# RWKV-7 time mixing: two solve copies one step later, one more weight ahead in two phases, the scan's second loads and its PSUM layout earlier

## The chip, the cores and the metric

The program runs on one core of a Trainium2 chip. The metric is the device time of one execution in microseconds (us), and a kernel's time is the median of its runs. Inside the core TensorE (PE) multiplies matrices, VectorE (DVE), ScalarE (ACT) and GpSimd (POOL) do the work by element, and SyncE (SP) issues most of the DMA transfers. Every engine works through its own instructions in a fixed order and stops at the first whose inputs are not there.

## The reference, cut to what matters

A decoder trunk of two layers on one sequence of 1024 positions, width 1024. Each layer has a token mixer, a cross-attention into 256 memory tokens and a squared-ReLU MLP, each with a norm ahead and behind. Layer 0 mixes by a gated linear recurrence, layer 1 by RWKV-7, which is what the change touches:

```python
xx = x_prev - x
r = (x + xx * mu[0]) @ w_rkv[0]
k = (x + xx * mu[2]) @ w_rkv[1]
v = (x + xx * mu[3]) @ w_rkv[2]
...
def step(state, inp):
    r_t, w_t, k_t, v_t, a_t, b_t = inp
    sa = jnp.einsum('bhij,bhj->bhi', state, a_t)
    state = state * w_t[:, :, None, :] + sa[..., None] * b_t[:, :, None, :] + v_t[..., None] * k_t[:, :, None, :]
    y_t = jnp.einsum('bhij,bhj->bhi', state, r_t)
    return state, y_t
```

There are 16 heads of 64. All numbers are float32.

## The kernel before

**Products in three parts.** A float32 product is made of three matmuls (mm3, L318 to L320): each operand is split into a rounded high part (ACT, L233) and a remainder (DVE, L234). So every weight and every activation passes through one ACT and one DVE instruction before PE can use it. A 128x128 block against 512 columns costs three matmuls.

**The order of work.** The program writes instructions down in an order; a planner then simulates the engines with its own durations, and issues on each engine what is ready, earliest written first. `with self.behind()` queues what is written in the block behind the last instruction written before it on each engine. A tile of the pool `u` (45 tiles of 128x1024) is handed out when the planner finds one free.

**The phases of layer 1's mixer** (function `rwkv`). After the low-rank maps come three phases, in which PE makes 8 blocks f = 0 to 7 of 128 features each, for k, then r, then v. `fphase` (L584 on) makes one block: 16 times three matmuls into the PSUM tile p, of which there are two, and then an evacuation: `prep_head` for k (ACT L1349, DVE L1350), `evac_r` for r (DVE L1519), `evac_v` for v (ACT L1553 and what follows). The input of each phase is a mix of x and its predecessor, `rwkv_make_mix`: in four steps for each half of the positions, ACT scales (L1217), DVE adds (L1220), and both split (L233, L234). The mix for r is made while k's blocks 6 and 7 are on PE and after them; the mix for v likewise at the end of the r phase. Mixes written into `self.later` are taken up in the middle of a block.

**Weights.** `take` (L262 on) hands out the next weight of a list known beforehand. At each call it issues loads up to `depth + ahead` weights beyond the one taken, and splits up to `depth` beyond it. In these phases DA = (2, 1), so two are split and one more is loaded.

**Aside steps.** Each block ends a step, numbered 0 to 6 for k (the last has blocks 6 and 7), 7 to 12 for r, 13 to 19 for v. `aside(step)` (L1488) places there the pieces of the chunk solve: the 64x64 triangular systems of all heads, in four groups q = 0 to 3. `solve_load` fetches a group, `solve` works through 31 dependent pairs of instructions (L1433, L1435), on POOL for q = 0, 1, 2 and on DVE for q = 3, and `solve_store` makes a transposed copy on ACT (L1445) and stores both (SP, L1446 and L1447). merge_load, merge and merge_store (steps 9 to 18) build the full inverses from these. The tuples SL, SO and ST give the steps of load, solve and store for q = 0 to 3.

**The scan.** 16 chunks c of 64 positions follow each other; a chunk's state update needs the chunk before. `load(n)` fetches the operands of chunks 2n and 2n+1: two `u` tiles by four DMAs (L1624), two halves of a z tile (L1627), and a `u` tile without a DMA; `load_solved(n)` the inverses (L1638, from what merge_store wrote), `load_late(n)` the values and gates (L1651, L1655). While chunk c runs, `scan_scale`, `scan_gram` (PE, L1679) and `scan_keys` prepare chunk c+1. Afterwards `tphase` multiplies by w_o into PSUM tiles p.

**PSUM.** "mixed" keeps four single banks (pool `still`) and two p tiles of two banks; "banks" turns the p tiles into four more banks. `bank(n)` takes from the one pool or from the other in turn. A pool can be laid out anew when the last reader of its old tiles is done.

Of the kernel before, what the change touches and what calls it, by code (L numbers as in the profile page):

```python
# [1141 lines left out]

TURNS = [[f] for f in range(6)] + [[6, 7]]

SL, SO, ST = (2, 5, 8, 9), (2, 5, 8, 9), (5, 8, 12, 13)
ML, ME, MS = range(9, 17), range(10, 18), range(11, 19)
SE = [lambda nc: nc.gpsimd] * 3 + [lambda nc: nc.vector]
MQ = lambda nc, f: nc.sync if f < 4 else nc.gpsimd
DA = (2, 1)
# [112 lines left out]
def rwkv(self, X, xt, lw_wa, lw_g, post, mid):  # L1262
# [116 lines left out]
    def sums(f):  # L1379

        ps = sm[f] = self.bank()
        for tt in range(8):
            self.between.append(lambda tt=tt: mm(ps[:, tt * 2:tt * 2 + 2], st_k[f][0][:, tt * 128:tt * 128 + 128], self.ind,
                                                 start=True, stop=True))
# [113 lines left out]
    for i, fs in enumerate(TURNS):  # L1498
        for f in TURNS[i + 1] if i < 6 else []:
            decay(f)  # L1500
        if len(fs) > 1:

            self.later.append(lambda: rwkv_make_mix(self, X, 0, 0, xr[0], range(2)))
        if i:
            sums(fs[0] - 1)
        self.fphase(I["b_w_rkv"][0, 1], fs, xk, prep)
        if 0 < i < 6:
            gram(fs[0] - 1)
        aside(i)
# [3 lines left out]
    def early(f):  # L1513
        ld[f] = self.unit()
        nc.sync.dma_start(ld[f], Pd[f * 128:f * 128 + 128, :])
# [6 lines left out]
    for i, fs in enumerate([[0, 1], [2], [3], [4], [5], [6, 7]]):  # L1522
        for f in fs:
            early(f)
        if i == 5:
            self.later.append(lambda: rwkv_make_mix(self, X, 3, 0, xv[0], range(3)))
        if i in (1, 2):
            sums(5 + i)
        self.fphase(I["b_w_rkv"][0, 0], fs, xr, evac_r, spread=i == 0)
        if i == 0:  # L1530
            prep_rest(7)
        if i in (1, 2):
            gram(5 + i)
        aside(len(TURNS) + i)
# [75 lines left out]
    def load(n):  # L1610

        if n >= 8:
            return
        ts = slice(n * 128, n * 128 + 128)
        if n in (0, 2):
            t = self.half_big([2, 8, 2, 128])
            mvb.extend(t[:, i] for i in range(2))
        mv = mvb[n % 4]
        sts = []
        for g in range(2):  # L1620
            st = self.unit().rearrange("p (e q w t) -> p e q w t", e=2, q=4, w=2)
            for e in range(2):
                es = slice(n * 128 + e * 64, n * 128 + e * 64 + 64)
                nc.sync.dma_start(st[:, e], STd[:, 4 * g:4 * g + 4, :, es])  # L1624
            sts.append(st)
        for w in range(2):
            nc.sync.dma_start(mv[:, :, w, :], MVd[:, :, w, ts])  # L1627
        pcs = self.unit().rearrange("p (e q t) -> p e q t", e=2, q=8)
        for e in range(2):
            c, cs = 2 * n + e, slice(e * 64, e * 64 + 64)  # L1630
            cst[c] = dict(st=[t[:, e] for t in sts], mv=mv[:, :, :, cs],
                          pcs=pcs[:, e], pcc=self.pc[:, c * 8:c * 8 + 8].unsqueeze(2), gw=[])

    def load_solved(n):
        if n >= 8:
            return
        xu = self.unit().rearrange("p (q t) -> p q t", t=128)
        nc.sync.dma_start(xu, XTd[:, :, n * 128:n * 128 + 128])  # L1638
        for e in range(2):
            cst[2 * n + e].update(xt=xu[:, :, e * 64:e * 64 + 64])  # L1640
# [101 lines left out]
    for i, fs in enumerate(turns):  # L1742
        for f in turns[i + 1] if i < 6 else []:
            early(f)
        if fs[-1] >= 5:
            self.depth, self.ahead = min(2, 7 - fs[-1]), 0
        self.fphase(I["b_w_rkv"][0, 2], fs, xv, evac_v, spread=i == 0)
        aside(len(TURNS) + 6 + i)
        if fs[-1] == LD:
            with self.behind():  # L1750
                load(0)
        if fs[-1] == 6:
            load_solved(0)
    for c in range(2):
        scan_scale(c)
        for g in range(2):
            scan_gram(c, g)
            scan_mask(c, g)
            scan_keys(c, g)
    load_late(0)  # L1760
    self.psum_layout("banks")
    for h in range(2):
        nc.gpsimd.memset(cst[0]["sv"][hr[h], :, h, :], 0.0)
    for c in range(16):
        if c % 2 == 0:
            with (ExitStack() if c else self.behind()):
                load(c // 2 + 1)
                load_solved(c // 2 + 1)
                load_late(c // 2 + 1)
        s = cst[c]  # L1770
        sv, mv, pcc, xtc, pcs = s["sv"], s["mv"], s["pcc"], s["xt"], s["pcs"]
        dbv = self.db[:, 0:128].rearrange("p (q a t) -> p q a t", a=2, t=8)[:, :, c % 2, c // 2:c // 2 + 1]
        W, U, S, wsb = [], [], [], []
        y = self.unit()
        yp = self.bank(c)
        Y = yp.rearrange("p (q i) -> p q i", i=64)

        def values(m):

            ph = self.bank(m)  # L1780
            reg = [ph[:, x * 256:x * 256 + 256].rearrange("p (q i) -> p q i", i=64) for x in range(2)]
            W.append(reg[0]); U.append(reg[1]); S.append(reg[0])
            for q, h in heads:
                mm(W[m][hr[h], q, :], s["gw"][m][:, q, h, 0:64], sv[:, m * 4 + q, h, :], start=True, stop=True)
            w_ = y[:, 512 + m * 256:768 + m * 256].rearrange("p (q i) -> p q i", i=64)
            nc.scalar.copy(w_, W[m])
            wsb.append(w_)

        def decayed(m):
            for h in range(2):  # L1790
                nc.gpsimd.tensor_tensor(pcs[hr[h], m * 4:m * 4 + 4, :], sv[hr[h], m * 4:m * 4 + 4, h, :],
                                        pcc[hr[h], m * 4:m * 4 + 4].broadcast_to([64, 4, 64]), ALU.mult)

        def from_state(m):
            for q, h in heads:
                mm(Y[hr[h], m * 4 + q, :], mv[hr[h], m * 4 + q, 1, :], sv[hr[h], m * 4 + q, h, :],  # L1796
                   start=(m == 0 and q == 0), stop=False)

        def solved(m):
            qs = slice(m * 4, m * 4 + 4)  # L1800
            for q, h in heads:
                mm(U[m][hr[h], q, :], xtc[hr[h], m * 4 + q, :], wsb[m][hr[h], q, :], start=True, stop=True)
            for h in range(2):
                nc.vector.tensor_tensor(sv[hr[h], qs, h, :], U[m][hr[h]], dbv[hr[h], qs].broadcast_to([64, 4, 64]), ALU.mult)

        def update(m):
            qs = slice(m * 4, m * 4 + 4)
            for q, h in heads:
                mm(S[m][hr[h], q, :], s["gk"][:, m * 4 + q, h, :], sv[:, m * 4 + q, h, :], start=True, stop=True)
            for h in range(2):  # L1810
                nc.vector.tensor_add(cst[c + 1]["sv"][hr[h], qs, h, :], pcs[hr[h], qs, :], S[m][hr[h]])

        def output():
            for m in range(2):
                for q, h in heads:
                    mm(Y[hr[h], m * 4 + q, :], s["gw"][m][:, q, h, 64:128], sv[:, m * 4 + q, h, :], start=False,
                       stop=(m == 1 and q == 3))
            nc.scalar.copy(y[:, 0:512], yp)
            s["y"] = y


        todo = [(decayed, 0), (decayed, 1)] if c < 15 else []
        if c:
            todo += [(scan_scale, c + 1)]
        todo += [(values, 0), (from_state, 0), (values, 1), (from_state, 1)]
        if c:
            todo += [(post_var, c - 1)]
        todo += [(solved, 0), (solved, 1)]
        if c > 1:
            todo += [(flip_out, c - 2)]  # L1830
        if c:
            todo += [(scan_gram, c + 1, 0)]
        if c < 15:
            todo += [(update, 0), (update, 1)]
        if c:
            todo += [(scan_keys, c + 1, 0), (scan_keys, c + 1, 1), (scan_mask, c + 1, 0), (scan_gram, c + 1, 1), (scan_mask, c + 1, 1)]
        todo += [(output,)]
        if c:
            todo += [(post_norm, c - 1)]
        for fn, *args in todo:  # L1840
            with self.line("scan"):
                fn(*args)
        if c > 4 and c % 2:

            n = (c - 3) // 2
            self.depth, self.ahead = max(0, n - 4), min(n, 4)
            self.fetch(self.taken - 1)
    post_var(15)
    post_norm(15)
    self.depth, self.ahead = 2, 3  # L1850
    self.psum_layout("mixed")

    self.later += [lambda: flip_out(14), lambda: flip_out(15)]
    w = I["b_w_o"][0]
# [54 lines left out]
```

## Time and profile before

| what | value |
|---|---|
| median of 3 runs (lowest to highest) | 2872.57 us (2865.99 to 2873.09) |
| the profiled execution's own time | 2871.51 us |
| its span, first to last instruction | 2869.8 us |
| granted TensorE clock over the span | 0.993 |
| PE busy / idle | 2779.0 us / 90.8 us |
| POOL solve of q = 0 / 1 / 2, first to last instruction | 1422.5 to 1476.6 / 1484.2 to 1540.9 / 1546.5 to 1588.4 |
| phases k, r, v on PE | about 1356 to 1486, 1489 to 1599, 1604 to 1749 |
| scan's chunks on PE | about 1762 to 1920 |

How to read the rows: a timeline row gives start and duration in us, the engine, the line, the operation, out<-in with shapes, and a count when neighbours are merged; in brackets stands the idle time of the engine just before, and what ended it. PEld is the weight load of a matmul, SPq the queue of SP, on which only DMA issues stand. A row of waits gives the total, the number and the longest. A row of a window gives busy time for each engine (with the number of instructions), the clock granted to PE, the mean busy share of the 16 DMA engines and GB/s. Tile names carry no numbers: u is the pool of 128x1024 tiles, p and q are PSUM, z the larger tiles, d scratch in DRAM.

### The profile page before, as it was taken

The page shows a single profiled execution, that of the slowest core. Times are in us where ns is not written, and L with a number is a line of the kernel's source. Part 1 is how long each engine was busy: PE and PEld are TensorE (multiplying, and loading weights), DVE is VectorE, ACT ScalarE, POOL GpSimd, SP SyncE. Part 2 cuts the span into 40 slices and gives each one's busy share as a digit, 9 for nine tenths or more (in the row PEclk, how much of TensorE's full clock was granted, in tenths as well). Part 3 has the DMA queues.
Part 4 walks back from the last instruction along what each step waited for, and adds up shares of the span by engine and source line. Part 5 has one row for each costly group of instructions (what it writes and reads, how often), then busy time and mean ns, then how long its engine had stood idle before and what let it go on. Part 6 is the DMA issues. An engine that isn't in the chain of part 4 may idle for free.

```text
span 2869.8 us, 42738 instructions
## 1 busy us (share of the span) xinstructions
PE 2779.0 (97%) x16955; PEld 2320.8 (81%) x16955; DVE 1845.2 (64%) x2004; ACT 1431.3 (50%) x2203; POOL 913.3 (32%) x962
## 2 busy tenths in 40 slices
PE   7999999999999999998999898999999999999998
PEld 6888788888888888887777687888888888888886
DVE  5577556557455577886575834785665655467778
ACT  5456344546544543438562544663463644555333
POOL 2000114023666500013188223863303276640001
PEclk9999999999999999999999999999999999999999
DMA  8212352323445654433557798963132255464453
GB/s 263 74 45 81 100 168 74 103 81 103 157 152 161 213 188 165 154 111 103 166 158 199 194 254 244 236 164 103 63 106 91 88 171 161 139 240 167 147 176 118
DMA packets 383592, 421.92 MB, mean 147 GB/s; under 512 B 91184, under 2 KB 294176, under 8 KB 383392
## 3 DMA queue, kind: packets, MB, share of 16 engines
q1 hardware_dynamic: 371360, 379.19, 43.7%
q0 software_dynamic: 11568, 39.41, 3.8%
q8 instruction: 133, 2.18, 0.3%
q14 instruction: 67, 0.55, 0.1%
q10 hardware_dynamic: 464, 0.59, 0.1%
HBM read 283.79 MB, written 134.74 MB: 146 GB/s over the span
## 4 chain that ended last, share of the span: by engine, by line
PE 81%; DVE 5%; POOL 3%; ACT 3%; DMA 3%; issue 3%; SPq 2%; ACTq 0%; DVEq 0%; POOLq 0%
PE q L318 17%; PE q L320 17%; PE q L319 17%; PE p L318 8%; PE p L320 8%; PE p L319 8%; PE q L1679 1%; DMA u<-d 1%; DVE u L234 1%; POOL u L1435 1%; ACT u L233 1%; DMA u<-in_b_w_rkv 1%; POOL w L1433 1%; PE q L1796 1%; ACT u L327 1%
## 5 line engine op out<-in xcount | busy, mean ns | idle before, releaser
L234 DVE TENSOR_TENSOR u<-u,u 128x1024 fp32r<-128x1024 f32 (+1 forms) x602 | 809.2, 1375 | 370.9 <-ACT u L233 342.2
L233 ACT CAST u<-u 128x1024 fp32r<-128x1024 f32 (+1 forms) x602 | 591.8, 1020 | 436.6 <-DVE u L1060 224.5
L318 PE MATMUL q<-u,u 128*128 128x512 f32 (+1 forms) x1952 | 744.2, 383 | 5.3 <-ACT u L233 2.4
L319 PE MATMUL q<-u,u 128*128 128x512 f32 (+1 forms) x1952 | 745.8, 382 | 0.5 <-POOL u L366 0.5
L320 PE MATMUL q<-u,u 128*128 128x512 f32 (+1 forms) x1952 | 740.4, 382 | 0.8 <-DVE u L234 0.8
L318 PE MATMUL p<-u,u 128*128 128x512 f32 (+1 forms) x1472 | 554.9, 379 | 18.9 <-DVE u L1519 5.6
L319 PE MATMUL p<-u,u 128*128 128x512 f32 (+1 forms) x1472 | 552.9, 376 | 3.6 <-DVE u L234 3.6
L320 PE MATMUL p<-u,u 128*128 128x512 f32 (+1 forms) x1472 | 552.2, 375 | 3.4 <-DVE u L234 3.4
L329 POOL TENSOR_SCALAR s<-s 128x1 f32<-128x1 f32 x98 | 43.1, 440 | 1268.6 <-ACT u L327 1266.9
L318 PEld LDWEIGHTS q<-u,u 128*128 128x128 f32 x1952 | 367.0, 188 | 77.3 <-ACT u L233 3.5
L320 PEld LDWEIGHTS q<-u,u 128*128 128x128 f32 x1952 | 366.9, 188 | 72.1 <-DVE u L234 1.0
L319 PEld LDWEIGHTS q<-u,u 128*128 128x128 f32 x1952 | 367.0, 188 | 71.6 <-POOL u L366 1.0
L318 PEld LDWEIGHTS p<-u,u 128*128 128x128 f32 x1472 | 280.8, 191 | 72.8 <-ACT u L233 10.6
L320 PEld LDWEIGHTS p<-u,u 128*128 128x128 f32 x1472 | 280.9, 191 | 55.0 <-DVE u L234 5.6
L319 PEld LDWEIGHTS p<-u,u 128*128 128x128 f32 x1472 | 280.9, 191 | 54.5 <-DVE u L234 7.6
L441 POOL TENSOR_TENSOR u<-u,u 128x512 f32<-128x512 f32 x120 | 186.0, 1555 | 8.9 <-PE q L319 5.1
L1118 DVE TENSOR_TENSOR z<-z,q 128x512 f32<-128x512 f32 x192 | 130.6, 683 | 80.9 <-PE q L320 80.9
L318 PE MATMUL q<-z,u 128*128 128x512 f32 x320 | 124.9, 390 | 1.6 <-ACT u L233 1.6
L319 PE MATMUL q<-z,u 128*128 128x512 f32 x320 | 124.5, 389 | 0.0
L320 PE MATMUL q<-z,u 128*128 128x512 f32 x320 | 124.2, 389 | 0.0
L442 POOL TENSOR_TENSOR u<-u 128x512 f32<-128x512 f32 x40 | 76.0, 1899 | 145.3 <-DVE u L234 73.1
L1015 POOL TENSOR_TENSOR u<-u,u 128x512 f32<-128x512 f32 x32 | 46.0, 1438 | 176.3 <-ACT u L1004 166.4
(250 smaller groups left out, 3332.7 us busy)
## 6 DMA issues: line engine op xcount, KB each, us to landing
u<-d SPq DMA_DIRECT2D x194, 512.0 KB, 4.7
d<-u SPq DMA_DIRECT2D x109, 512.0 KB, 3.3
d<-u POOLq DMA_DIRECT2D x68, 512.0 KB, 3.5
d<-u SPq DMA_DIRECT2D x132, 256.0 KB, 3.7
u<-in_m_w_up SPq DMA_DIRECT2D x64, 512.0 KB, 5.4
u<-in_m_w_down SPq DMA_DIRECT2D x64, 512.0 KB, 7.9
u<-in_c_w_kv SPq DMA_DIRECT2D x32, 512.0 KB, 6.4
u<-in_b_w_rkv SPq DMA_DIRECT2D x24, 512.0 KB, 6.7
```

The costliest lines, as they stand in the source:

```text
L233: self.nc.scalar.copy(hv, src)
L234: (eng or self.nc.vector).tensor_tensor(lv, src, hv, ALU.subtract)
L318: mm(o, ah, bh, start=first, stop=False, **kw)
L319: mm(o, ah, bl, start=False, stop=False, **kw)
L320: mm(o, al, bh, start=False, stop=last, **kw)
L327: nc.scalar.activation(junk, src, AF.Square, accum_out=ss)
L329: nc.gpsimd.tensor_scalar(v, ss, 1.0 / n, eps, ALU.mult, ALU.add)
L441: sub = lambda o, x, y: nc.gpsimd.tensor_tensor(o, x, y, ALU.subtract)
L442: nc.gpsimd.tensor_tensor(s[:, a], f1[:, a], f1[:, b], ALU.add)
L1015: tt(s1, r21, r22, ALU.add)
L1118: nc.vector.tensor_add(to_, to_, o)
L1433: eng.tensor_tensor(tv, xv_[:, 0:n, s:s + 1].broadcast_to([128, n, m]), Lv[:, s:s + 1, s + 1:].broadcast_to([128, n, m]), ALU.mult)
```

## The change

Four edits, all in layer 1's mixer. (1) ST goes from (5, 8, 12, 13) to (6, 9, 12, 13): the copies and stores of solves q = 0 and q = 1 are written one step later. (2) During k's block 5 and r's block 5 `ahead` is 2 instead of 1, so that block 1's weight of the next phase is loaded (not split) one step earlier. (3) load(1) is written after the v phase's block 6 instead of at chunk 0, and load_solved(1) right behind the v phase. (4) The PSUM layout goes back to "mixed" when chunk 15 begins, instead of after it.

```diff
-SL, SO, ST = (2, 5, 8, 9), (2, 5, 8, 9), (5, 8, 12, 13)
+SL, SO, ST = (2, 5, 8, 9), (2, 5, 8, 9), (6, 9, 12, 13)
...
             sums(fs[0] - 1)
+        self.depth, self.ahead = DA if i != 5 else (DA[0], DA[1] + 1)
         self.fphase(I["b_w_rkv"][0, 1], fs, xk, prep)
...
             sums(5 + i)
+        self.depth, self.ahead = DA if i != 4 else (DA[0], DA[1] + 1)
         self.fphase(I["b_w_rkv"][0, 0], fs, xr, evac_r, spread=i == 0)
...
         if fs[-1] == 6:
             load_solved(0)
+            load(1)
+    with self.behind():
+        load_solved(1)
     for c in range(2):
         scan_scale(c)
...
     for c in range(16):
+        if c == 15:
+            self.psum_layout("mixed")
         if c % 2 == 0:
             with (ExitStack() if c else self.behind()):
-                load(c // 2 + 1)
-                load_solved(c // 2 + 1)
+                if c:
+                    load(c // 2 + 1)
+                    load_solved(c // 2 + 1)
                 load_late(c // 2 + 1)
...
     self.depth, self.ahead = 2, 3
-    self.psum_layout("mixed")
```

## The prediction

> **What bounds the kernel now.** I read the page's first rows, then PE's waits in the changed mixer (1350 to 1925 us), then the timelines of PE, DVE, ACT and SP around each of them.
>
> ```profile
> span 2869.8 us, 42738 instructions
> PE 2779.0 (97%) x16955; PEld 2320.8 (81%) x16955; DVE 1845.2 (64%) x2004; ACT 1431.3 (50%) x2203; POOL 913.3 (32%) x962
> PE p L318 <- DVE u L1519: 5.6, 3, 3.6
> PE q L1679 <- DMA u<-d: 5.5, 1, 5.5
> PE p L319 <- DVE u L234: 2.9, 5, 0.7
> PE p L318 <- DVE u L1350: 2.1, 1, 2.1
> ```
>
> PE is busy for 2779.0 of 2869.8 us. The 90.8 us of idle are the whole stock, and no edit touches PE's own work. The last four rows (total, number, longest) are what the edits can reach: 16 us, in three places: the seam from k to r, the seam from r to v, and the scan's start. The 2.9 us that hang on DVE's splits say that at a seam DVE, which makes the next phase's input, sets the end and not PE.
>
> **Seam k to r (ST of q = 0, weight r1).** What stands in the way now:
>
> ```profile
> 1476.62 2.06 ACT L1445 COPY u<-u 64x1024 f32<-64x1024 f32 x1 [11.26 <-POOL u L1435]
> 1479.67 2.36 DVE L234 TENSOR_TENSOR u<-u,u 128x1024 fp32r<-128x1024 f32 x2 [10.93 <-ACT u L233]
> 1481.94 2.73 DVE L1220 SCALAR_TENSOR_TENSOR u<-z,colt,u 128x511 f32<-128x511 f32 x4
> 1484.59 2.48 DVE L234 TENSOR_TENSOR u<-u,u 128x1024 fp32r<-128x1024 f32 x2
> 1484.45 2.08 PE L1405 MATMUL q<-u,u 64*64 64x64 f32 x64
> 1487.36 2.29 DVE L1350 TENSOR_TENSOR u<-u,p 128x1024 f32<-128x1024 f32 x2
> 1488.66 0.51 PE L318 MATMUL p<-u,u 128*128 128x512 f32 x1 [2.13 <-DVE u L1350]
> ```
>
> The copy of q = 0 stands on ACT for 11.26 us behind POOL's solve; what is queued behind it on ACT, the splits and scalings of the mix for r, waits too, and DVE idles 10.93. One step later the copy is out of the way: ACT goes on at 1465.4, and DVE does its 2.36 + 2.73 + 2.48 = 7.57 us of splitting and mixing before 1478. Not all of that is won. The last evacuation needs k's block 7, whose matmuls end where L1405 begins, at 1484.45. DVE's half of an evacuation is 2.29 / 2 = 1.15, and ACT's half I put at the same, so the second L1350 can end at about 1486.8; now it ends at 1487.36 + 2.29 = 1489.65. Behind it DVE works on the mix without a hole, and r's first two blocks end with that mix. So the seam moves by 2.85; I take **2.7**, as two or three splits won't fit as tightly. Bounds: 0, if the rest of the mix is laid where it was; 5.3, if DVE doesn't bind and all PE waits around it go (2.13, three for L234, 2.0 together, and one of 1.2 for L1519). A loss is possible: if the 7.57 land behind L1350 instead, 7.57 − (1489.65 − 1484.59) = 2.5 us later.
>
> r1's raw weight earlier serves only an ACT that arrives earlier: it is part of this seam and costs nothing beside a DMA issue (below). The copy of q = 1 waits now too; PE works throughout, and no row of PE answers to it: 0, bounds 0 and 1, one short L319 wait.
>
> **Seam r to v (weight v1, ST of q = 1).**
>
> ```profile
> 1573.39 0.43 SPq L249 DMA_DIRECT2D u<-in_b_w_rkv  x1
> 1588.80 1.41 SPq L249 DMA_DIRECT2D u<-in_b_w_rkv  x2
> 1596.70 1.05 ACT L233 CAST u<-u 128x1024 fp32r<-128x1024 f32 x1 [12.27 <-DMA u<-in_b_w_rkv]
> 1597.78 1.22 DVE L234 TENSOR_TENSOR u<-u,u 128x1024 fp32r<-128x1024 f32 x1 [6.68 <-ACT u L233]
> 1602.70 1.22 DVE L1519 TENSOR_TENSOR u<-u,p 128x1024 f32<-128x1024 f32 x1
> 1604.07 0.47 PE L318 MATMUL p<-u,u 128*128 128x512 f32 x1 [3.63 <-DVE u L1519]
> 1606.23 2.06 ACT L1445 COPY u<-u 64x1024 f32<-64x1024 f32 x1
> ```
>
> v0 goes out at 1573.39, v1 15 us later. ACT waits 12.27 us for v1, DVE 6.68 for ACT's part of its split, so r's block 6 is evacuated late and PE idles 3.63. Issued right behind v0, with the 1596.70 − 1588.80 = 7.9 us that it now takes to land, v1 is there at about 1582, before ACT asks for it at 1584.4. DVE's 6.68 go, and PE's 3.63 with them. Afterwards ACT has copies that wait for PE (which gained 3.63) and the mix for v is not 6.68 but about 5 us earlier: PE's 3.63 and the 1.3 of short waits for splits that follow in v's first blocks. I take **4.9**; bounds 0 (no tile is free for v1 any earlier) and 6.7.
>
> **SP.** The stores of q = 0 and 1, and the earlier weights, now stand in SP's order ahead of other issues of their steps, the merge loads and L1515's, which r's evacuation reads. The rows above show 0.43 to 0.7 us for an issue; two stores and a weight are about 1.5. I take a loss of **1.0** in all; bounds 0 and 1.5 at each seam, 3.
>
> **The scan's second loads.**
>
> ```profile
> 1740.00:1750.00 10.00, 9.02 (x40) 7.13 (x38) 2.54 (x4) 2.33 (x4) 5.85 (x8) 1.00 0.61 182
> 1770.00:1780.00 10.00, 4.46 (x90) 4.03 (x85) 1.69 (x4) 2.39 (x17) 1.63 (x3) 0.78 1.05 243
> ```
>
> ```profile
> 1751.93 2.44 SPq L1577 DMA_DIRECT2D u<-u  x4
> 1768.55 0.64 PE L1784 MATMUL q<-u,u 128*64 128x64 f32 x16
> 1770.65 6.49 SPq L1624 DMA_DIRECT2D u<-d  x4
> 1777.50 2.08 PE L1679 MATMUL q<-z,u 64*128 64x128 f32 x16 [5.54 <-DMA u<-d]
> 1785.02 0.78 PE L1784 MATMUL q<-u,u 128*64 128x64 f32 x16
> 1794.68 0.81 PE L1784 MATMUL q<-u,u 128*64 128x64 f32 x16
> ```
>
> PE waits 5.54 us for load(1)'s four L1624, which SP issues only at 1770.65, with the DMA engines full (share 1.05). From one L1784 to the next, chunk 1 takes 1785.02 − 1768.55 = 16.47 us and the following one 1794.68 − 1785.02 = 9.66: 6.8 too much, 5.54 of them the wait and the rest slow matmuls at a granted clock of 0.78. Written behind v's block 6, the loads go out while the DMA engines are at 0.61. On SP they stand ahead of L1577's copies for chunk 0 (1751.93), which they delay by up to their own 6.49 us if they go out as late as that, with PE not yet in the scan. What comes next is L1651 for chunk 2, at SP behind the same loads now, and so earlier by about 6.49. I take **6.0**, between the 5.54 and the 6.8; lower bound 0, if load(1)'s u tiles come free only at chunk 0, as an issue at 1770.65 could also mean.
>
> **PSUM at chunk 15.**
>
> ```profile
> 1910.80 1.15 PE L1816 MATMUL q<-u,u 128*64 128x64 f32 x32
> 1917.67 2.04 PE L1816 MATMUL q<-u,u 128*64 128x64 f32 x32
> 1919.62 1.22 DVE L234 TENSOR_TENSOR u<-u,u 128x1024 fp32r<-128x1024 f32 x1
> 1920.64 0.50 PE L318 MATMUL p<-u,u 128*128 128x512 f32 x1 [0.92 <-ACT u L1818]
> ```
>
> The last chunk's L1816 takes 2.04 in place of 1.15, and 0.92 of idle follow: 1.8 in all. But the next matmuls also need the split that DVE ends at 1920.84, and chunk 15 itself now has four banks in place of eight. I take **0.3**; bounds −0.6 (a pause as long as a short wait for a split, 2.9 / 5) and 1.8.
>
> **Sum.** 2.7 + 4.9 − 1.0 + 6.0 + 0.3 = 12.9. The profiled execution took 2871.51 us, 1.7 more than its span: 2871.5 − 12.9 = 2858.6. The median of the three runs, 2872.57, is 1.06 above it, so 2859.7; the forecast is **2860.0**. 0.3%, about what a measurement of this kernel can tell from no change, is 8.6 us: faster is below 2864.0, slower above 2881.2.
>
> **Rivals.** *The seams give nothing* (0.18). DVE has no hole behind L1350 and L1519; if the planner fills the freed stretch with other DVE work, the mix ends where it does now. Left are 6.0 + 0.3 − 1.0 = 5.3: 2867. Against it: 10.93 and 6.68 us of DVE standing still just ahead of the seams.
>
> *PE's clock counts at the seams* (0.10). The clock granted around the two gaps:
>
> ```profile
> 1486.00:1496.00 10.00, 7.87 (x44) 6.32 (x40) 9.97 (x12) 8.44 (x12) 9.06 (x13) 0.83 0.02 1
> 1602.00:1612.00 10.00, 7.93 (x86) 5.96 (x87) 9.70 (x14) 7.76 (x11) 0.00 (x0) 0.83 0.34 138
> ```
>
> At 0.83 of the clock, 10 us do the work of 8.3: 1.7 us behind each gap. The sum leaves them out, as DVE (9.97 and 9.70 busy) sets the pace there. If PE sets it, they come on top, with 0.8 more in the scan: 12.9 + 4.2 = 17.1, so 2856. [...]
>
> *POOL's solves slip* (0.06). DVE's early mix now runs beside solve(0). A step of one shape is slower beside a busy DVE (the second) than beside an idle one:
>
> ```profile
> 1476.31 0.28 POOL L1435 TENSOR_TENSOR u<-u,w 128x31 f32<-128x31 f32 x1
> 1587.99 0.40 POOL L1435 TENSOR_TENSOR u<-u,w 128x31 f32<-128x31 f32 x1
> ```
>
> By these the 8.6 us of solve from 1468 to 1476.6 stretch by 0.12 / 0.28, 3.7 us. The solve of q = 2 ends at 1588.39, and ACT would reach its copy at about 1596.9, now 1606.23: 8.5 us of slack. Beyond that ACT stands inside the mix for v and the 4.9 are lost: 2865. [...]
>
> *No effect* (0.10). Tiles and planner leave loads and steps where they are: 2872.6. For it: a `u` tile is handed out when one is free, wherever the load is written. Against it: at 1588.80 two weights go out at once.
>
> *Slower* (0.14): the 45 tiles of u run out. A raw weight, the solved tiles and load(1)'s four are held a step longer; from the point where none is free for an input tile of the next phase, at 1465 and at 1574, the early mix is laid behind the evacuations. That costs the 2.5 above at k to r; at r to v four halves of a mix and two splits, 2.73 + 2 x 1.22 = 5.2; with SP's 1.0 and nothing won in the scan 8.7: 2881.3. For it: the pair at 1588.80, as if both had waited for a tile. Against it: late in a phase its weights free tiles block by block.
>
> **How the numbers follow.** The forecast has 0.42, with a range of its own of 2854 to 2866 (seams at 9.6 in place of 7.6 and the scan's 6.8; seams at about 2). Of it 0.36 lie below 2864; with 0.09 of the clock, 0.03 of the seams and 0.02 of POOL, faster has 0.50. Slower has 0.11 of the last rival and 0.01 of no effect, 0.12. The rest, 0.38, is within 0.3%. From 2852 to 2875 the range takes in all cases but the slower one (0.13 of it) and about 0.05 at its ends.
>
> **What would show it.** Right: ACT's copy of q = 0 with little or no wait and DVE's 10.93 gone; PE's 2.13 ahead of r gone; ACT's 12.27 for v1 gone and PE's 3.63 under 0.5; L1624 of chunks 2 and 3 issued before 1760, no wait at L1679, chunk 1 near 10 us; the last L1816 still near 2.0. Wrong: a new wait for a weight or for POOL at a seam; L1350 or L1519 late behind mixes; merge loads late on SP; L1577 late at the scan's start; a wait for L1651 in chunk 2 in place of the one removed.

## The result, and the profile after

The changed kernel takes 2861.85 us (median of 10 runs, 2856.90 to 2870.38), the kernel before beside it 2872.17 (10 runs). The ratio is 0.9969 with a 95% interval of 0.9958 to 0.9979: 6 to 12 us faster. The forecast was 2860.0. That is 12.2 below the median of before, at the upper end of the 6 to 12. The profiled execution took 2859.99 us, 11.5 less than that of before.

The head of the changed kernel's page. Lines from L1506 on have moved: L1516 was L1515, L1520 and L1521 were L1519 and L1520, L1590 was L1588, L1681 was L1679, L1792 was L1784, L1810 was L1802, L1824 was L1816.

```profile
span 2858.3 us, 42737 instructions
PE 2778.7 (97%) x16955; PEld 2321.7 (81%) x16955; DVE 1846.3 (65%) x2004; ACT 1431.1 (50%) x2203; POOL 915.2 (32%) x962
```

PE's waits in it from 1350 to 1925 us (total, number, longest):

```profile
PE p L319 <- DVE u L234: 3.5, 4, 1.6
PE q L1472 <- DMA u<-d: 3.2, 1, 3.2
PE q L1810 <- issue: 2.3, 2, 1.8
PE q L1792 <- DMA u<-d: 2.1, 2, 1.6
PE p L318 <- DVE u L1520: 1.3, 1, 1.3
```

PE's work is the same. Gone are L1350's 2.1 and the 5.5 for the scan's loads, and of the 5.6 for r's evacuation (L1519, now L1520) 1.3 are left. New are 3.2 for the merge's loads (0.95 before) and 2.1 for the values of chunk 2.

At the seam from k to r, timelines of ACT, DVE and POOL:

```profile
1488.60 1.11 ACT L1349 ACTIVATE u<-p,nkk 128x1024 f32<-128x1024 f32 x1 [4.57 <-PE p L320]
...
1471.11 3.00 DVE L234 TENSOR_TENSOR u<-u,u 128x1024 fp32r<-128x1024 f32 x2
1474.03 3.54 DVE L1220 SCALAR_TENSOR_TENSOR u<-z,colt,u 128x511 f32<-128x511 f32 x4
1489.75 1.22 DVE L1350 TENSOR_TENSOR u<-u,p 128x1024 f32<-128x1024 f32 x1 [4.46 <-ACT u L1349]
...
1481.59 0.28 POOL L1435 TENSOR_TENSOR u<-u,w 128x31 f32<-128x31 f32 x1
```

ACT now waits for PE's blocks and not for POOL. DVE does the early mix from 1471 on, and its last evacuation stands for PE's last block. The solve of q = 0 ends at 1481.87, 5.3 us later than before (0.8 of it since it also began later), and DVE's own instructions are stretched too (3.54 for what took 2.73).

At the merges (PE, then SP) and at the scan's start (PE, then SP):

```profile
1577.96 1.88 PE L1472 MATMUL q<-u 32*32 32x32 f32 x62 [3.16 <-DMA u<-d]
...
1603.94 0.50 PE L318 MATMUL p<-u,u 128*128 128x512 f32 x1
...
1557.24 0.35 SPq L1446 DMA_DIRECT2D d<-u  x1
...
1558.56 0.81 SPq L1459 DMA_DIRECT2D u<-d  x1
...
1571.53 1.96 SPq L1458 DMA_DIRECT2D u<-d  x4
1575.06 1.97 SPq L249 DMA_DIRECT2D u<-in_b_w_rkv  x2
...
1764.58 1.16 PE L1681 MATMUL q<-z,u 64*128 64x128 f32 x16
1772.16 0.30 PE L1792 MATMUL q<-u,u 128*64 128x64 f32 x2 [1.63 <-DMA u<-d]
1772.97 0.65 PE L1792 MATMUL q<-u,u 128*64 128x64 f32 x14 [0.52 <-DMA u<-d]
...
1734.84 4.43 SPq L1626 DMA_DIRECT2D u<-d  x4
1761.09 3.81 SPq L1657 DMA_DIRECT2D u<-d  x2
1764.95 3.84 SPq L1653 DMA_DIRECT2D u<-d  x4
```

v0 and v1 go out together at 1575.06, and PE has no gap ahead of v (1603.94, where it idled 3.63). load(1)'s four loads go out at 1734.84, 36 us sooner, and L1681 waits no more. But chunk 2 waits 1.63 + 0.52 for its values, L1653, which stand on SP behind 3.81 us of gate loads.

**Where PE gained and lost.** The table shows by how many us PE began the same instruction later (+) or earlier (−) than in the trace of before, worked out from the timelines of PE, one profiled execution each. The columns are the changed kernel and the experiments of the next section.

```
PE's place                   before  changed no load(1)  ST alone  weights  load(1)  PSUM
last matmul of k            1484.13   +4.05      +1.96     -0.62    -0.47    -1.13  +2.38
in r's block 2              1522.59   -0.04      -0.58     -6.21    -1.86    -1.68  +1.93
in r's block 5              1562.30   -0.32      -0.85     -6.50    -2.14    -1.97  +1.69
last matmul of r            1598.92   +3.58      +2.92     -0.92    -0.80    +1.88  +2.85
in v's block 2              1641.95   -6.54      -6.51     -3.95    -7.41    -4.34  +1.62
gate products, last but few 1739.01   -7.56      -8.78     -3.80    -8.74    -5.87  +4.68
the one after               1739.33   -7.41      -6.43     -3.64    -2.94    -3.60  +4.68
start of chunk 3            1794.68  -12.50      -4.64     -4.24    +0.52    -8.32  +4.47
start of chunk 15           1912.38  -11.33      -5.66     -4.03    -1.37    -8.24  +1.77
17 matmul groups after scan 1933.30  -11.51      -5.84     -4.01    -1.38    -8.25  +1.58

PE's place             values first  block 7  q=1 at 8  merge loads  ST+merge  merge+values  all
last matmul of k              +1.53    +0.71     +4.29        +1.73     -0.06         -0.04  +1.90
in r's block 2                -1.97    -4.85     +0.28        -0.36     -3.44         -4.93  -0.67
in r's block 5                -2.26    -5.12     +0.00        +0.83     -2.27         -3.86  +0.41
last matmul of r              +1.25    +1.93     +4.47        +6.34     +6.26         +5.70  +5.26
in v's block 2                -6.67    -5.44     -6.07        -4.95     +3.77         -5.58  -5.22
gate products, last but few   -9.32    -6.46     -3.70        -3.45     +6.44         -5.74  -4.12
the one after                 -7.04    -6.46     -3.70        -2.49     +6.44         -5.22  -4.12
start of chunk 3             -14.68    -8.01     -8.64        -6.43     +7.41        -12.92 -11.93
start of chunk 15            -11.09   -10.61    -10.26        -5.39     +5.50        -10.54 -11.77
17 matmul groups after scan  -11.26   -10.79    -10.44        -5.58     +5.49        -10.73 -11.96
```

Single traces differ by some us where nothing was changed: load(1) and PSUM alone are the same program as before up to v's last blocks, and stand at −4.34 and +1.62 in v's block 2. So one column proves little; what repeats over many weighs more. In the changed kernel PE gains 4.1 from the end of k to r's block 2, loses 3.9 from r's block 5 to the end of r, gains 10.1 from there to v's block 2, and 5.1 at the scan's start.

In these traces PE loses time in two ways, by idling and by a lowered clock. The first two stretches in windows (width, then PE's busy time; the clock granted to PE is third from the right): from the end of k to r's block 2 in before, the changed kernel and ST alone, then from r's block 5 to the end of r in before and the changed kernel:

```profile
1484.10:1522.60 38.50, 33.18 (x218) 26.48 (x217) 38.43 (x36) 25.30 (x36) 35.61 (x37) 0.92 0.42 108
1488.20:1522.60 34.40, 30.20 (x218) 24.43 (x217) 32.85 (x29) 25.04 (x34) 31.89 (x33) 1.00 0.44 121
1483.50:1516.40 32.90, 30.22 (x218) 24.41 (x217) 31.32 (x29) 25.05 (x34) 28.70 (x32) 1.00 0.49 140
...
1562.30:1598.90 36.60, 34.89 (x385) 28.12 (x384) 24.34 (x39) 8.93 (x14) 23.19 (x38) 1.00 0.73 194
1562.00:1602.50 40.50, 37.34 (x386) 30.33 (x384) 33.80 (x51) 16.66 (x21) 24.55 (x38) 0.92 0.73 197
```

At the seam idle time falls from 5.3 to 4.2 and 2.7 us, and the clock's share, 0.08 of 38.5 or 3.1 us, goes in both. Inside r idle time grows from 1.7 to 3.2, and 0.08 of 40.5, another 3.2 us, goes to a lower clock that before did not have there. In both stretches the clock moves more of the time than the waits do in the changed kernel.

### The profile page after: what moved, and what is told of

The parts are those of the page before. It is cut to its first block, busy times and chain, and to the rows that moved or that the text cites. A ratio compares the mean times of both kernels' runs of the same rounds, so it can differ in the third digit from the quotient of the medians.

```text
span 2858.3 us, 42737 instructions
## 1 busy us (share of the span) xinstructions
PE 2778.7 (97%) x16955; PEld 2321.7 (81%) x16955; DVE 1846.3 (65%) x2004; ACT 1431.1 (50%) x2203; POOL 915.2 (32%) x962
## 5 line engine op out<-in xcount | busy, mean ns | idle before, releaser
L234 DVE TENSOR_TENSOR u<-u,u 128x1024 fp32r<-128x1024 f32 (+1 forms) x602 | 809.1, 1375 | 345.0 <-ACT u L233 326.0
L318 PE MATMUL q<-u,u 128*128 128x512 f32 (+1 forms) x1952 | 744.2, 383 | 5.3 <-ACT u L233 2.4
L318 PE MATMUL p<-u,u 128*128 128x512 f32 (+1 forms) x1472 | 554.1, 379 | 12.4 <-ACT u L948 5.8
L318 PEld LDWEIGHTS q<-u,u 128*128 128x128 f32 x1952 | 366.9, 188 | 77.6 <-ACT u L233 3.5
L318 PEld LDWEIGHTS p<-u,u 128*128 128x128 f32 x1472 | 280.1, 190 | 65.1 <-ACT u L948 6.7
L318 PE MATMUL q<-z,u 128*128 128x512 f32 x320 | 124.9, 390 | 1.6 <-ACT u L233 1.6
```

The lines of the kernel that those rows point to most:

```text
L234: (eng or self.nc.vector).tensor_tensor(lv, src, hv, ALU.subtract)
L318: mm(o, ah, bh, start=first, stop=False, **kw)
```

## The experiments

### Each part alone

The four edits, each by itself on the kernel before (the diffs are those of the change). ST:

> Only ST changed: the copies and stores of q = 0 and q = 1 one step later. The forecast's terms: 2.7 us off at the seam from k to r, about 1.0 back on SP, nothing else: about 1.7 us faster than before, PE's 2.13 wait ahead of r gone, r1's weight (as late as before) waited for by ACT but not by PE; the 3.63 ahead of v stays. In the changed kernel PE waited 3.16 us (0.95 before) at L1472 for the merge's loads. Rival A: the stores of q = 1, now in front of the merge loads on SP, are the cause; then a wait of about 3 us at L1472 shows here too, and the seam's 2.7 are lost again: no difference from before. Rival B: the second raw weight on the DMA queues is the cause; then L1472's wait stays under 1.5 here.

Measured: 2871.37 us, ratio 0.9995 (0.9986 to 1.0005): no difference. PE's waits from 1350 to 1925 us:

```profile
PE q L1472 <- DMA u<-d: 4.4, 2, 3.5
```

PE is 6.2 us ahead in r's block 2, with the 2.13 gone; at the end of r 0.9 are left, and L1472 waits 3.5 and once more 0.9. So rival A's wait is there without a second weight. In the trace the seam's gain exists, and it is given back inside r. By the times the forecast's 1.7 is not excluded: the interval goes from 4 us faster to 1.4 slower.

The weights:

> Only the weights of the next phase one step earlier (k's and r's block 5). The forecast's terms: nothing at k to r, as ACT still stands at the copy for 11 us; 4.9 us off at r to v, so about 4.9 faster. From the changed kernel's trace: the seam r to v is worth about 6.4 and the first blocks of v another 3 (waits of 0.88 and 2.84 at the gate's products). Rival A (stores cause the merge's wait): L1472 waits about 1 us as before, in all about 9 us faster. Rival B (two raw weights beside the merge's loads): L1472 waits 3 us and the slow clock behind it costs as much again: about 5 to 6 us faster, by accident the forecast's number.

Measured: 2867.33, ratio 0.9980 (0.9971 to 0.9990), 3 to 8 us faster, the forecast's 4.9 in the middle. L1472 waited 1.7, between the two rivals' 1 and 3. The trace holds a loss that nobody expected, late in v (PE's waits; then DVE and POOL):

```profile
PE q L1590 <- DVE u L234: 5.6, 1, 5.6
```

```profile
1729.42 1.28 DVE L1562 SCALAR_TENSOR_TENSOR u<-u,colt,u 128x1024 f32<-128x1024 f32 x1 [6.85 <-DMA u<-d]
1730.63 5.70 DVE L234 TENSOR_TENSOR u<-u,u 128x1024 fp32r<-128x1024 f32 x1
...
1730.65 4.02 POOL L1670 TENSOR_TENSOR u<-u,pc 128x512 f32<-128x512 f32 x4
```

A split that took 1.22 us here in the changed kernel takes 5.70 while POOL scales the scan's first operands, and POOL loses nothing by it. PE, 8.74 ahead until then, stands at 2.94 behind it.

load(1):

> Only load(1) and load_solved(1) earlier. The forecast's term: 6.0 us faster, chunk 1 near 10 us, PE's 5.54 at L1679 gone. Rival: part of it comes back, as the values and gates of chunk 2 (L1651, L1655) still go out at chunk 0 and PE waits for them; the changed kernel shows 1.63 + 0.52 there: then 4 to 5 us.

Measured: 2870.53, ratio 0.9990 (0.9977 to 1.0002): 2.9 us by the ratio, and neither zero nor the forecast's 6.0 is excluded. The 5.54 is gone, 2.1 + 0.4 at the values are new, and from v's last gate product to chunk 3 PE gains 4.7: the rival's 4 to 5 by the scan's own stretch. The same split of DVE took 2.15 us here, and PE waited 2.1 at L1588.

PSUM:

> Only the PSUM layout at chunk 15. The forecast's term: 0.3 us faster, no more than the measurement can tell. The PE idle of 0.92 ahead of the first p matmul goes. Rival: it only moves, to the split of the first weight (0.5 in the changed kernel), and four banks make chunk 15 slower: 0 to 1 us slower.

Measured: 2873.29, ratio 1.0002 (0.9992 to 1.0012). Between the start of chunk 15 and a place behind the scan PE gains 0.19 us here (1.77 to 1.58) and 0.18 in the changed kernel: the forecast's 0.3 nearly, and no more than nothing by the times. Over the same stretch all nine traces with this edit gain 0.17 to 0.20, and the four others that are not before move by 0.02 or less. The timeline of PE in this run:

```profile
1922.65 0.50 PE L320 MATMUL p<-u,u 128*128 128x512 f32 x1 [0.51 <-DVE u L234]
```

L1816's block is as long as before (2.04 us), the 0.92 are gone, and 0.51 for the split of the first weight came in their place.

### The changed kernel without load(1)

```diff
             load_solved(0)
-            load(1)
-    with self.behind():
-        load_solved(1)
...
-                if c:
-                    load(c // 2 + 1)
-                    load_solved(c // 2 + 1)
+                load(c // 2 + 1)
+                load_solved(c // 2 + 1)
```

> The changed kernel without load(1) and load_solved(1) earlier; edits 1, 2 and 4 stay. The forecast's terms: 6.0 us slower than the changed kernel, about 6.9 us faster than before. If load(1) is worth what it showed alone (about 2 to 3 us by the times): 2 to 3 slower than the changed kernel. From the trace of the scan: 5.4 of PE's wait come back, less the 2.15 that load(1) left at L1792: 4 to 5 slower by the scan's own stretch; what the times show beyond or below that comes from the v phase ahead of it.

Measured: 2866.14, ratio 0.9981 (0.9968 to 0.9993). That is 4.3 us slower than the changed kernel by the medians and 3.4 by the ratios; the intervals of the two overlap. The three other edits are worth 5.5 us by the ratio, where the forecast had 6.9 for them. By the middle values load(1) is worth less than 6.0, in company (3.4 to 4.3) as alone (2.9), but the intervals are wide enough for 6.0.

### The values ahead of the gates

```diff
     def load_late(n):
...
+        if n:
+            load_gates(n)
...
                 load_late(c // 2 + 1)
+                if not c:
+                    load_gates(0)
```

load_gates(n) holds L1657's two loads, so that chunk 0's and chunk 1's gates now go out behind the values of chunks 2 and 3.

> The changed kernel with one order turned round at the scan's start: SP issues the values of chunks 2 and 3 (L1653) ahead of the gates of chunks 0 to 3 (L1657), which chunk 0 and 1 don't need before their output. Theory: load(1) was worth less than the forecast's 6.0, since chunk 2 then waits for its values (1.63 + 0.52 us at L1792 in the changed kernel), which stand on SP behind two gate loads of 3.8 us; then this wait goes to under 0.5 and the kernel is about 2 us faster than the changed one. Rival: the DMA engines are full there (share 1.1) and the order doesn't matter; then the wait stays at 1.5 or more.

Measured: 2861.83, ratio 0.9964 (0.9951 to 0.9977). The theory is right on the wait; the time doesn't show it. SP and PE:

```profile
1760.97 5.74 SPq L1653 DMA_DIRECT2D u<-d  x4
...
1770.73 0.64 PE L1801 MATMUL q<-u,u 128*64 128x64 f32 x16
```

PE's waits:

```profile
PE q L1819 <- issue: 3.6, 2, 2.1
...
PE q L1590 <- DVE u L234: 2.1, 1, 2.1
```

L1801 (L1792 in the changed kernel) starts chunk 2 with no wait, and from v's last gate product to chunk 3 PE gains 7.6, the forecast's 6.8 with more. But 2.1 went to the split beside POOL ahead of the scan, and 3.6 to waits of PE within the scan that the trace puts down to no engine. In the median nothing remains; by the intervals 2 us are not excluded.

### The operands of v's block 7 one block sooner

```diff
-        for f in turns[i + 1] if i < 6 else []:
+        for f in turns[i + 1] + [7] * (i == 4) if i < 5 else []:
             early(f)
```

> The changed kernel with the operands of v's block 7 (L1603, L1605) loaded one block sooner. In the run with only the weights ahead, a split of DVE (L234) took 5.70 us in place of 1.22 while POOL ran L1670 and PE waited 5.6 us at L1590; alone with load(1), 2.15 and PE 2.1; in the changed kernel the same split ended just as POOL began. Theory: this is a race between that split, which stands behind an instruction that waits for those operands, and POOL's work, and it costs some runs of the changed kernel 5 us; then with the operands sooner the split ends 3 to 4 us before POOL begins, the slow runs go, and the kernel is 1 to 2 us faster in the median. Rival: the race is rare in the changed kernel; then the split moves and the time doesn't.

Measured: 2861.71 (2860.49 to 2865.48), ratio 0.9966 (0.9954 to 0.9977). DVE and POOL:

```profile
1728.32 1.23 DVE L234 TENSOR_TENSOR u<-u,u 128x1024 fp32r<-128x1024 f32 x1 [3.47 <-ACT u L233]
...
1732.94 4.04 POOL L1670 TENSOR_TENSOR u<-u,pc 128x512 f32<-128x512 f32 x4
```

The split ends 3.4 us before POOL begins, and takes 1.23. The two are apart, but the median doesn't move: this trace has 3.17 for the values of chunk 2 and 4.6 + 1.3 for the merges. Eight runs without one above 2866 are not enough to say that the highest of the changed kernel's times (2870) came from this race.

### The store of q = 1 back at step 8

```diff
-ST = (6, 9, 12, 13)
+ST = (6, 8, 12, 13)
```

> The changed kernel with the copy and store of q = 1 at step 8, as before; q = 0 stays at 6. Theory A: the stores of q = 1, in front of the first merge loads on SP, and the second raw weight behind them make PE wait at L1472 (3.16 in the changed kernel and 3.5 with ST alone, 0.95 to 2.9 where ST is as before); then this wait falls to 2 or less and the kernel is 1 to 3 us faster than the changed one. Rival B: any gain at the seam from k to r is given back there, since the merge's loads stand on SP behind a store that waits for r's own evacuation and land a fixed time after it; then the wait stays near 3 and the time is the same.

Measured: 2862.26, ratio 0.9971 (0.9958 to 0.9984): the same as the changed kernel. L1472 still waits 3.0 + 0.3. The two stores take 1.3 us of SP ahead of the first merge loads, and the issues right behind them are slower too (L1459 and L1460 take 0.81 and 1.58 in the changed kernel, 0.43 and 0.49 in before): from L1417 to the operand of r's evacuation (L1516, in before L1515) SP takes 7.6 us in the changed kernel, 4.7 here and 4.8 in before. So they do hold SP up; but without them the wait is the same. From the issue of the next merge loads (L1458) to PE's L1472 it is 6.1 us here, 6.4 in the changed kernel and 4.8 in before. Theory A falls for the wait, and its 1 to 3 us did not come. B's account of the wait was tried next.

### The merge's loads one step sooner

```diff
-ML, ME, MS = range(9, 17), range(10, 18), range(11, 19)
+ML, ME, MS = (8, 9, 10, 11, 13, 14, 15, 16), range(10, 18), range(11, 19)
```

On the changed kernel:

> The changed kernel with the loads of the first four merges one step sooner (ML 8, 9, 10, 11, then 13 to 16), so that on SP they no longer stand behind the stores of q = 1 and behind the store that waits for r's evacuation. In eight traces PE waited 0.95 to 4.6 us at L1472 for these loads, and what PE had won or lost at the seam from k to r was gone behind them. Theory G: this wait is a loss of its own, and with the slow clock behind it 3 to 4 us; then it goes under 0.5 and the kernel is 3 to 4 us faster than the changed one. Theory S: the delay is covered by the next bound, DVE's mix for v: where PE came late through the merges it found no gap ahead of v, where it came early it waited 3.63; then the wait goes and the time stays within 1 us, as PE waits ahead of v or in its first blocks.

Measured: 2865.34, ratio 0.9975 (0.9966 to 0.9985): 3.5 slower than the changed kernel by the medians, which neither theory had, and 1.7 by the ratios, whose intervals overlap: a loss is not shown, a gain of 3 to 4 us did not come. DVE, SP and PE:

```profile
1575.69 1.22 DVE L1520 TENSOR_TENSOR u<-u,p 128x1024 f32<-128x1024 f32 x1 [7.67 <-DMA u<-d]
...
1567.07 2.03 SPq L1458 DMA_DIRECT2D u<-d  x4
1570.26 1.72 SPq L1516 DMA_DIRECT2D u<-d  x1
...
1572.96 1.17 PE L1472 MATMUL q<-u 32*32 32x32 f32 x62 [0.66 <-DMA u<-d]
1576.97 0.74 PE L318 MATMUL p<-u,u 128*128 128x512 f32 x1 [2.84 <-DVE u L1520]
1587.58 0.80 PE L318 MATMUL p<-u,u 128*128 128x512 f32 x1 [1.92 <-DVE u L1520]
```

L1472's wait fell to 0.66. But the operand of r's evacuation, L1516, goes out only at 1570.26 (1564.34 in the changed kernel), behind the merge's loads; DVE waits 7.67 for it, the p tile is free that much later, and PE waits 2.84 and 1.92. SP's one queue feeds the merges and the evacuations, and with the loads set forward another on it went out 5.9 us later.

On ST alone:

> Before with ST changed and the loads of the first four merges one step sooner; weights, scan and PSUM as before. ST alone: PE was 6.5 us ahead in r's block 4 (2 to that where ST is as before) and 0.9 ahead of v's first block. If the seam's gain is given back at the merge's loads and nowhere else: PE keeps about 5 us to the end, 4 to 5 us faster than before. If it is given back at whatever comes next: PE waits for v1's weight or the mix ahead of v (3.63 in before, 5 or more here), and the kernel is 1 to 2 us faster, as with ST alone.

Measured: 2876.30, ratio 1.0010 (1.0001 to 1.0019): slower than before. PE's waits:

```profile
PE p L318 <- DVE u L1519: 6.8, 4, 2.5
...
PE p L319 <- DVE u L234: 4.7, 6, 1.2
```

This pair shows what v1's earlier weight does. At the end of r PE is 6.3 late in both runs (+6.34 and +6.26). In v's block 2 the run with the weights ahead stands at −4.95, the one without at +3.77: 8.7 us between them. With v1 in place the mix for v goes on while PE is late, and PE finds it ready; without it, ACT and DVE wait with PE. The sooner merge loads and ST are in both, and load(1) and PSUM act later, so the weights make the difference. The other traces bear this out: in v's block 2 all nine with the weights stand at −4.95 to −7.41, the four without at −4.34 to +3.77, and before at 0.

Two more, both on the changed kernel, with the values ahead of the gates, and in the second block 7's operands sooner too:

> The changed kernel with the merge loads one step sooner and the values of chunks 2 and 3 ahead of the gates on SP. If both waits were losses of their own (3 to 4 and 2 us): 2856. If the first is covered by the mix for v and the second by the collision of DVE and POOL in v (which cost 2.1 in the run with the order of values and gates alone): 2860 to 2862, no different from the changed kernel.

> As the run before it, with the operands of v's block 7 also one block sooner, which took the split of DVE away from POOL's work but left PE 3.2 us of waiting for the values of chunk 2. With the values now ahead of the gates that wait should go: by the sum of what the traces showed 2854 to 2857, the fastest of all. If the waits cover each other: 2860 to 2862.

Measured: 2861.02 (0.9967, 0.9954 to 0.9979) and 2861.78 (0.9968, 0.9956 to 0.9981). Both have the waits for the evacuation that the sooner merge loads bring (6.0 and 4.9 us at L318), and neither is any different from the changed kernel. The 2854 to 2857 of the sum did not come, and no version here beats the changed kernel.

## Why the prediction was right, point by point

The total was forecast as 12.9 off the profiled execution, and 11.5 were measured there; by the ratio of the runs it is 8.9, by the medians 10.3. Each by itself, the edits gave by their ratios 1.4 (ST), 5.7 (weights), 2.9 (load(1)) and −0.6 (PSUM), 9.4 together, each good to 3 or 4 us; of these only the weights' gain is clear of zero. The parts of the forecast stand less well than the sum: a loss on SP taken too small and a gain in the scan taken too large stand against gains at the seams that were larger in the traces. That the sum came so near the profiled execution is in part luck.

**Seam k to r: the waits as forecast, the clock left out.** The copy no longer waits, DVE mixes early, and the last evacuation is bound by PE's last block of k: ACT's L1349 waits 4.57 for PE, and DVE's L1350 comes right behind. From the end of k to r's block 2 PE gains 4.1 in the changed kernel, 5.6 in ST alone and 5.6 with block 7 sooner, where load(1), weights and PSUM alone have 0.5 to 1.4: some 3 to 4.5 against the forecast's 2.7. By the windows 1.1 to 2.6 of this is idle time, and 3.1 the clock. The forecast left the clock out here, since DVE sets the pace, and gave it to a rival. DVE was busy for 38.43 of 38.50 us in before, so PE at full clock might only have waited longer for it; how the gain divides between DVE and the clock stays open.

**SP: the step that failed in size.** The forecast gave 1.0 for issues that stand in front of others, and named the merge loads and L1515. From r's block 5 to the end of r, the changed kernel lost 3.9, ST alone 5.6, the other four with ST at (6, 9) or (6, 8) and no change of the merges' steps 3.5 to 7.1 (no load(1), values first, block 7, q = 1 at 8). But PSUM and weights alone, where ST is as before, lost 1.2 and 1.3, and load(1) alone 3.9: part of the loss belongs to no edit. In the changed kernel it is 1.5 more of idle and 3.2 of the lower clock behind the wait (0.72 from 1574 to 1586, where before had 1.00); the forecast had nothing for the second. The stores of q = 1 hold SP up by 2.8 us (7.6 against 4.8), more than the forecast's upper bound of 1.5 for a seam, but the run with q = 1 at step 8 has the wait without them. The merge's loads follow PE's gain, but not by all of it: with ST alone PE is 6.5 us ahead in r's block 5, SP issues L1458 2.7 sooner (1567.20 against 1569.85), and PE starts on what they bring 1.6 sooner (1573.09 against 1574.69). Why it is 4.8 us in one trace and 6.4 in another from that issue to PE's start, on programs that are equal up to there (before, load(1) alone), stays open.

**Seam r to v: right, and more than it said.** 4.9 was forecast, and the run of the weights alone gives 5.7 by its ratio. In the trace the gain is 10.1 from the end of r to v's block 2, which also gives back what PE had lost at the merges. The forecast took r's blocks and this seam as two terms to be added; they cover each other. That is why e.g. 6.3 lost in r cost the changed kernel with sooner merge loads so little, and how the sum could be right while SP's term was not. From the start of the k phase (+1.11 in the changed kernel, +0.36 without load(1)) to v's block 2, the changed kernel gains 7.7 and the one without load(1) 6.9; the forecast for the two seams and SP was 6.6. But load(1) alone, whose program up to there is that of before, gains 4.0 on the same stretch, so this nearness may be chance.

**The scan's loads: the wait right, the gain too high.** The 5.54 went, and the loads went out where the forecast put them. It named L1651 as the next to be late and took it to move up by as much as the loads before it. It did move, from 1778.36 to 1764.95 (now L1653), by 13.4 us, but the chunk that needs it moved by nearly as much, from 1785.02 to 1772.16: 2.15 of waiting are left. With that, 5.54 to 6.8 become 3.4 to 4.7, and the runs show 2.9 alone and 3.4 to 4.3 in company. The run with the values first shows that their place behind the gates causes the wait; that the wait is what the time lacks is argued, since in that run the wait went and the time stayed.

**PSUM: right.** 0.3 forecast, 0.2 in the traces, not to be told from zero by the times.

**The rivals.** POOL's solve of q = 0 slipped by 5.3 us, more than the rival's 3.7; that of q = 2 ended 1.05 later (1589.44 against 1588.39), and ACT came to its copy only at 1598.75, without a wait. The tiles did not run out: v1 went out with v0, load(1) at 1734.84. Slower than before was only ST with the merge loads moved. Two of the forecast's own signs of being wrong appeared all the same: merge loads late on SP, and a wait for the values in chunk 2.

## What to carry to other kernels

Ask of each wait that is to be removed what PE meets next, and whether a later bound already covers it: two waits in a row are not two terms of a sum, and a delay ahead of work that is made independently of PE cost little here (with the merge loads sooner PE was 6.3 us late at the end of r and 4.95 ahead in v's block 2). Put an operand early on a shared in-order queue only after reading what stands behind it; moving the merge's loads by one step brought a new wait elsewhere (6.0 us at L318) and no gain. Count behind a wait the clock as well: inside r the lower clock cost the changed kernel 3.2 us, more than the 1.5 by which its idle time grew. Where one profiled execution is compared with one other, first look how far apart two traces of the same stretch of program are; here it was 6 us in v's block 2, as much as the largest term.

## What the runs showed of the hardware

**DVE and POOL side by side.** In four of the traces the split L234 began within 0.2 us of POOL's L1670. Once DVE was held to 5.70 us and POOL ran at its usual 4.02; three times (values first, without load(1), load(1) alone) DVE took 2.06 to 2.15 and POOL 5.04 to 5.13. Apart, they take 1.22 and 4.02. The 5.70 are about the sum of the two: 1.22 and POOL's four instructions of 1.0, with 0.5 over. What stands behind this no run shows. Within 0.2 us who started first did not settle which of the two takes longer: at 5.70 DVE's record began 0.02 us before POOL's. With the merge loads sooner DVE began 0.38 us ahead, took its 1.22, and POOL's four took 4.73.

**PE's clock without a gap.** Two windows of the changed kernel, 10 us each, with PE (the first of the busy times) busy all the time, and the clock in the third column from the right:

```profile
1435.00:1445.00 10.00, 10.00 (x103) 8.26 (x102) 8.10 (x9) 8.17 (x10) 9.29 (x10) 0.83 0.61 147
1455.00:1465.00 10.00, 10.00 (x100) 8.21 (x100) 6.37 (x7) 8.21 (x11) 9.31 (x9) 0.83 0.59 159
```

In before both had 1.00. At 0.83 each costs 1.7 us, 3.4 together; PE falls back by 2.9 between the start and the end of k in this trace (+1.11 to +4.05). Both hold small matmuls (L1383, 128x128 against 2 columns, and L1405, 64x64). In the run with PSUM alone, whose program there is that of before, the second window had 0.83 as well: the same program had the dip in one execution and not in another. Just ahead of the first window PE had idled for 0.67 us, and in before for 0.87 at the same place, without a dip. What brings the dip on, no run tested.
